# Hybrid diffusion layer on one core: the modulation's rest moved behind the scan, twelve low parts moved to VectorE, shared rows for the exponents

## Chip, cores and metric

One core of a Trainium2 chip runs the whole program. The metric is the device time of one execution in microseconds (us); the kernel before has a median of 1192.13 us over three runs (1191.94 to 1193.13). Engines: TensorE (PE), VectorE (DVE), ScalarE (ACT), GpSimd (POOL) and SyncE (SP), whose queue issues all DMAs.

## What is computed

One layer over 512 latent tokens and 256 context tokens of width 1024, all in float32:

```python
shift1, scale1, gate1, shift2, scale2, gate2 = jnp.split(c_mod[:, None, :], 6, axis=-1)
h = modulate(rms_norm(x, norm1), shift1, scale1)
u = h @ w_in                                   # q, k, v of A and C, z, xbc, dt of B, three gates
...
xs, bm, cm, dt = ssm_inputs(lat('b_xbc'), lat('b_dt'), ssm_conv_w, ssm_conv_b, ssm_dt_bias)
yf, _ = ssd_scan(xs, dt[:, :, 0], a_coef[0], bm, cm, hf_c, True)
yb, _ = ssd_scan(jnp.flip(xs, 1), jnp.flip(dt[:, :, 1], 1), a_coef[1],
                 jnp.flip(bm, 1), jnp.flip(cm, 1), hb_c, True)
ys = ssm_output(yf, jnp.flip(yb, 1), xs, lat('b_z'), ssm_d, ssm_norm)
x = x + gate1 * merge_branches(ya, ys, yg, lat('gates'), w_oa, w_ob, w_oc, w_out)
h2 = modulate(rms_norm(x, norm2), shift2, scale2)
x = x + gate2 * conv_ffn(h2, ffn_w_up, ffn_w_gate, ffn_conv_w, ffn_conv_b, ffn_w_down)
```

Branch A is sliding-window attention, branch C dense attention, branch B a state-space scan that runs forward and backward over chunks of 128 tokens. c_mod is silu(c) @ w_mod + b_mod: six vectors of 1024. shift1 and scale1 are needed first; gate1, shift2, scale2 and gate2 ("the rest of the modulation") are needed only after the three branches are merged.

## The kernel before

Every matrix product is made of three float32r products: each operand is split into a high and a low part (hi and lo, `split`), and hi x hi, hi x lo and lo x hi are summed in PSUM. For weights `wchunk` loads 128x1024 floats (512 KB) into raw, ScalarE copies them into whi, and raw - whi is written to wlo by VectorE or, where its second argument is `pool`, by GpSimd.

**Order.** The code records operations with `Plan`, which then simulates them with a table of durations (`_Eng`, `HOP`, `RELEASE`) and issues, engine by engine, the order it found. `ph(prio, lane, side, dma)` sets priorities for what is recorded next (TensorE, the other engines, DMAs; a smaller number goes first), and `P.hold` makes operations depend on another one. On the chip each engine, and SP's queue, works through its list strictly in order, and waits where an operand is not there.

**Stages, in the order of the profile's time.**
- 0 to 60 us: first modulation (`mod1`, f32r parts mh and ml), normalization and transposes of x, then k, v and q of branch C (`kv_proj`, `q_proj`) and the context tokens (tiles ch and cl; cl is made by GpSimd).
- to 400 us: attention of C and A (`att_unit`: scores in S, exponentials p, their parts ph and pl, products with V), with the convolved inputs of the scan (`xbc_tile`) and `dt_part` as filler.
- 400 to 560 us: `z_part` (weights' low parts on GpSimd), the chunk states of the scan (tiles H, xwh, xwl, yac) and the first gates of `merge`.
- 560 to 700 us: `scan_g` for two groups of heads and four chunks each. Per half chunk of four heads TensorE computes exponents into S (two matmuls per direction: one of SL with SR, one of idr with a mask), ScalarE takes the exponential E, VectorE and ScalarE scale it and make Mh and Ml, and TensorE multiplies xhl by these. Per chunk VectorE adds the result to yac and multiplies by zg, ScalarE squares it (ssB), TensorE transposes yac, and VectorE makes yn, then yth and ytl.
- 427 to 800 us: `merge` for branches C, A and B: per column block of 128 a gate product (hh, hl with w_g) and an output product (y0, y1, yth, ytl with the branch's weights), into m32. What does not depend on the scan runs beside it.
- 700 to 840 us: merge of B's remaining blocks, w_out, second norm; then the MLP to the end.

**The rest of the modulation.** `mod_rest(gi)` (lines 1024 to 1054) handles one of four vectors in two halves. For each half VectorE forms acc, the sum over eight rows of weights times sc, from four loads mraw of 512 KB, and TensorE sums acc over partitions (with a matrix of ones). The gates (gi 0 and 3) go through DRAM (gsc) and come back as g1 and g2; shift2 and scale2 go to md2. acc and mraw have one buffer each, in the pool wp. For gi 0 to 2 it is called behind `xbc_tile` with `P.hold = {mark[7]}` (the last product of the second unit of C's attention) and priorities 4.5, 2.8, 1.85.

**The exponents.** Two pairs of tiles SR and SL are kept. For each direction, SR has the sums of the four heads in rows 0 and 1 (high and low part) against ones in SL's rows 0 and 1, and SL's rows 2 to 9 have the same sums against -1 in SR, so that their product is the difference of the sums at two positions. They come from DRAM tiles fsc0 and fsc1:

```python
for d in range(2):
    f = fsc[d][c, g * 2 + q]
    sync.dma_start(SR[q][0:2, d].bitcast(F32).rearrange("s (h t) -> s h t", h=4), f.rearrange("(s h) t -> s h t", s=2))
    sync.dma_start(SL[q][2:10, d].bitcast(F32), f)
    pe.matmul(ps[:, d], SL[q][:, d], SR[q][:, d], start=True, stop=False)
    pe.matmul(ps[:, d], idr, bc(mkr[:, d], 1, [128, 4, 128]), start=False, stop=True)
```

Of the kernel before, what the change touches and what calls it, by code (L numbers as in the profile page):

```python
# [9 lines left out]
F32 = mybir.dt.float32  # L10
# [369 lines left out]
RELEASE = 0.2  # L380
HX = 0.0
# [21 lines left out]
class _Eng:  # L403
# [3 lines left out]
    def __getattr__(self, m):  # L407
        def call(*args, **kw):
# [9 lines left out]
            if self._n == "pe":  # L418
                n = int(np.prod(out.shape[1:]))
                if m == "transpose" or args[1].dtype == F32:  # L420
                    dur = 109.0 if m == "transpose" else max(108.0, n * 1.667 + 2.5)
                else:
                    dur = max(57.0, n * 0.436 + 4.0)
                if not kw.get("start", True):
                    reads.append(out)
            elif self._n == "dma":
# [3 lines left out]
                dur, lat = n * 4 / 360.0, 2200.0  # L430
            else:
# [18 lines left out]
                if self._n == "act" and "accum_out" in kw:  # L450
                    dur += 205.0
# [14 lines left out]
def emit(tc, A, dbg=None):  # L466
    P = Plan(tc)
# [275 lines left out]
    def kv_proj(br, hold0=set(), hold1=set()):  # L743
        P.hold = hold0
        chs = [wchunk(A["w_kv"][br * 2 + i], pool) for i in range(2)]
# [35 lines left out]
    def q_proj(br, u, early=None):  # L781
        if early is not None:
            ph(QP, "proj", 0.4, early)
        chs = [wchunk(A["w_q"][(br * 2 + u) * 2 + i], pool) for i in range(2)]
# [102 lines left out]
    fsc = [T(dr, [4, 4, 8, 128], F32, f"fsc{d}") for d in range(2)]  # L887
# [56 lines left out]
    def dt_part():  # L944
# [40 lines left out]
        for d, mi in ((0, "U"), (1, "Lo")):  # L985
            pf = bank((128, 4, 128))
            for c in range(4):
                pe.matmul(pf[0:16, c], dA[:, c, d * 16:d * 16 + 16], M[mi], start=c == 0, stop=c == 3)
            fh, fl = ftile((128, 4, 128), F32R), ftile((128, 4, 128), F32R)
            split(fh[0:16], fl[0:16], pf[0:16])  # L990
            for j, f in enumerate((fh, fl)):
                for gq in range(4):
                    sync.dma_start(fsc[d][:, gq, j * 4:j * 4 + 4, :].rearrange("c h t -> h c t"), f[gq * 4:gq * 4 + 4].bitcast(F32))
# [30 lines left out]
    def mod_rest(gi):  # L1024

        for hf in range(2):
            acc = T(wp, [128, 512], F32, "acc", bufs=1)
            for c4 in range(4):
                raw = T(wp, [128, 1024], F32, "mraw", bufs=1)
# [62 lines left out]

    ytp = openp("ytp", bufs=1, side="right")
# [69 lines left out]
    sg1 = T(ss2, [128, 128], F32, "G", bufs=2)  # L1163
    sync.dma_start(sg1, A["segc"][:, 512:640])
# [4 lines left out]
    SR = [T(ss2, [128, 2, 512], F32R, f"SR{i}") for i in range(2)]  # L1169
    SL = [T(ss2, [128, 2, 128], F32R, f"SL{i}") for i in range(2)]  # L1170
    for i in range(2):
        act.activation(SR[i], bc(sgc, 1, [128, 2, 512]), AF.Copy)
        act.activation(SL[i], bc(sg1, 1, [128, 2, 128]), AF.Copy)
    ssB = T(cst, [128, 4, 2], F32, "ssB")
    def scan_g(g):
# [10 lines left out]
        for c in range(4):  # L1186
# [42 lines left out]
            act.activation(zg, y, AF.Square, accum_out=ssB[:, c, g:g + 1])  # L1229

# [72 lines left out]
    closep("ytp")  # L1303
    closep("yp")
# [85 lines left out]

    ap = openp("ap", bufs=1, side="left")
# [5 lines left out]
    mod_rest(3)  # L1397
# [73 lines left out]
def lay_out(x, c, ctx, c_ctx, w_mod, b_mod, norm1, norm2, w_in, a_sink, ssm_conv_w, ssm_conv_b, ssm_A_log, ssm_dt_bias,  # L1471
# [108 lines left out]
```

## Time and profile before

| | |
|---|---|
| median of 3 runs | 1192.13 us |
| the profiled execution: its time, its span | 1197.12 us, 1195.3 us |
| TensorE busy, mean granted clock | 1132.8 us, 0.978 |
| VectorE, ScalarE, GpSimd busy | 809.4, 557.8, 276.9 us |
| DMA | 133.49 MB, mean 112 GB/s |

The time of a run includes a little before and after the span. All rows of the trace come from this one execution. Almost every instruction has the same line (456, where operations are recorded), so tiles tell them apart: b and S are tiles in PSUM, f is the filler's tile, and a name such as b<-whi,hh is output<-inputs. An idle time in brackets is that of the engine before the instruction, with what ended it. The granted clock is a share of TensorE's 2.4 GHz; at the lower of its two levels, 1.2 GHz, it is 0.5.

### The profile page before, as it was taken

How to read it: one execution, taken by the hardware profiler on the slowest of the kernel's cores; microseconds unless marked ns; L12 is line 12 of the kernel's file. 1: busy time of each engine (PE TensorE's matmuls, PEld its weight loads, DVE VectorE, ACT ScalarE, POOL GpSimd, SP SyncE). 2: the span in 40 equal slices, each digit the busy share in tenths (PEclk: the TensorE clock that was granted, in tenths of full speed). 3: DMA queues.
4: the chain of work that ended last, by engine and by line, in shares of the span. 5: the costliest groups of instructions: out<-in, count | busy, mean ns of one | idle time of the engine just before them, and what ended most of it. 6: DMA issues, size and time to landing. Idle time of an engine off the chain costs nothing.

```text
span 1195.3 us, 16560 instructions
## 1 busy us (share of the span) xinstructions
PE 1132.8 (95%) x6218; PEld 956.8 (80%) x6218; DVE 809.4 (68%) x1231; ACT 557.8 (47%) x1017; POOL 276.9 (23%) x181
## 2 busy tenths in 40 slices
PE   6989999899999999999999679999999999999996
PEld 1779888898888998777888568888988888888885
DVE  3788998868997668898898755435865555552423
ACT  4635787347775533435665523236433333332222
POOL 0455232342232453652332200024000000000100
PEclk8999999899999999999999779999999999999999
DMA  8610010331111675546233212352553323233321
GB/s 302 225 62 27 23 63 1 107 124 54 41 54 58 180 239 191 195 153 196 84 113 103 72 53 89 97 185 71 181 171 90 104 90 104 91 123 106 96 80 71
DMA packets 52047, 133.49 MB, mean 112 GB/s; under 512 B 5184, under 2 KB 17600, under 8 KB 51968
## 3 DMA queue, kind: packets, MB, share of 16 engines
q1 hardware_dynamic: 51968, 132.44, 34.1%
q8 instruction: 49, 0.80, 0.3%
q14 instruction: 30, 0.25, 0.1%
HBM read 122.06 MB, written 10.35 MB: 111 GB/s over the span
## 4 chain that ended last, share of the span: by engine, by line
PE 83%; DVE 8%; ACT 4%; issue 2%; DMA 1%; POOL 1%; SPq 0%; POOLq 0%; DVEq 0%; ACTq 0%
PE b L456 73%; PE S L456 11%; DVE pl L456 1%; DVE f L456 1%; DVE st L456 1%; ACT E L456 1%; DVE acc L456 1%; DMA mraw<-in_w_m 1%; DVE y L456 1%; ACT whi L456 0%; DVE yac L456 0%; DVE E L456 0%; DMA m<-in_w_m 0%; DMA SL<-fsc 0%; DVE wlo L456 0%
## 5 line engine op out<-in xcount | busy, mean ns | idle before, releaser
L456 ACT ACTIVATE whi<-raw 128x1024 fp32r<-128x1024 f32 x146 | 154.5, 1059 | 267.7 <-PE b L456 207.1
L456 DVE TENSOR_TENSOR wlo<-raw,whi 128x1024 fp32r<-128x1024 f32 x112 | 140.4, 1254 | 173.8 <-ACT whi L456 173.7
L456 PE MATMUL b<-h2h,whi 128*128 128x512 f32 (+1 forms) x400 | 145.2, 364 | 1.8 <-ACT h2h L456 1.8
L456 PE MATMUL b<-h2l,whi 128*128 128x512 f32 (+1 forms) x400 | 145.5, 364 | 0.6 <-DVE h2l L456 0.5
L456 PE MATMUL b<-h2h,wlo 128*128 128x512 f32 (+1 forms) x400 | 145.8, 366 | 0.0
L456 PE MATMUL b<-hh,whi 128*128 128x512 f32 x288 | 114.4, 397 | 2.1 <-DVE m L456 0.9
L456 PE MATMUL b<-hh,wlo 128*128 128x512 f32 x288 | 114.5, 397 | 0.0
L456 PE MATMUL b<-hl,whi 128*128 128x512 f32 x288 | 114.3, 397 | 0.0
L456 POOL TENSOR_TENSOR wlo<-raw,whi 128x1024 fp32r<-128x1024 f32 x34 | 86.0, 2540 | 112.8 <-ACT whi L456 111.3
L456 PE MATMUL b<-wlo,hh 128*128 128x256 f32 x320 | 92.3, 290 | 1.9 <-POOL wlo L456 1.9
L456 PE MATMUL b<-whi,hh 128*128 128x256 f32 x320 | 93.2, 292 | 0.0
L456 PE MATMUL b<-whi,hl 128*128 128x256 f32 x320 | 92.0, 289 | 0.0
L456 PEld LDWEIGHTS b<-h2h,whi 128*128 128x128 f32 x400 | 75.2, 189 | 14.3 <-ACT h2h L456 2.0
L456 PEld LDWEIGHTS b<-h2l,whi 128*128 128x128 f32 x400 | 75.4, 189 | 12.9 <-DVE h2l L456 1.1
L456 PEld LDWEIGHTS b<-h2h,wlo 128*128 128x128 f32 x400 | 75.3, 189 | 12.4 <-issue 0.5
L456 POOL TENSOR_TENSOR x<-x,fn 128x512 f32<-128x512 f32 x4 | 5.6, 1399 | 293.3 <-ACT f L456 293.3
L456 POOL TENSOR_TENSOR p<-p,st 128x768 f32<-128x768 f32 (+2 forms) x32 | 43.4, 1357 | 119.0 <-DVE st L456 99.3
L456 PEld LDWEIGHTS b<-wlo,hh 128*128 128x128 f32 x320 | 62.6, 196 | 2.6 <-POOL wlo L456 2.1
L456 PEld LDWEIGHTS b<-hh,whi 128*128 128x128 f32 x288 | 54.3, 189 | 13.0 <-DVE m L456 1.3
L456 PEld LDWEIGHTS b<-whi,hl 128*128 128x128 f32 x320 | 62.4, 196 | 0.9 <-issue 0.9
L456 PEld LDWEIGHTS b<-whi,hh 128*128 128x128 f32 x320 | 62.6, 196 | 0.7 <-issue 0.2
L456 PE MATMUL S<-kT,qT 128*128 128x256 f32 (+2 forms) x256 | 61.1, 340 | 2.1 <-ACT p L456 1.2
(287 smaller groups left out, 2866.6 us busy)
## 6 DMA issues: line engine op xcount, KB each, us to landing
mraw<-in_w_m SPq DMA_DIRECT2D x32, 512.0 KB
raw<-in_w_g SPq DMA_DIRECT2D x24, 512.0 KB
raw<-in_w_up SPq DMA_DIRECT2D x22, 512.0 KB
raw<-in_w_gate SPq DMA_DIRECT2D x22, 512.0 KB
raw<-in_w_down SPq DMA_DIRECT2D x22, 512.0 KB
m<-in_w_m SPq DMA_DIRECT2D x16, 512.0 KB
xg<-xsc SPq DMA_DIRECT2D x28, 256.0 KB
raw<-in_w_x SPq DMA_DIRECT2D x12, 512.0 KB
```

What stands on the lines that cost most here:

```text
L456: return f(*[res(a) for a in args], **{k: res(v) for k, v in kw.items()})
```

## The change

Five things are changed. (1) `mod_rest` for gi 0 to 2 is called behind `scan_g`, held until the square of the seventh of eight chunks (`ydone[MH]`), with priorities 6.5, 7.2 and 5.5; its tiles lie in a pool of its own, mrp (m3p for the fourth), with two buffers for mraw. (2) The low parts of the four k, v chunks and eight q chunks are made by VectorE. (3) fsc is one tensor; SR has no direction any more and holds the sums of both directions in rows 0 to 3, SL picks the direction by its ones and zeros; three loads per half chunk and not four. (4) Some of the planner's durations are other numbers. (5) Two small loads use other tiles.

```diff
+MH = 6
+MD = 5.5
...
-                    dur = 109.0 if m == "transpose" else max(108.0, n * 1.667 + 2.5)
+                    dur = 109.0 if m == "transpose" else max(224.0, n * 1.75)
...
-                    dur = max(57.0, n * 0.436 + 4.0)
+                    dur = max(111.0, 120.0 if n == 256 else n * 0.436 + 4.0)
...
-                dur, lat = n * 4 / 360.0, 2200.0
+                dur, lat = n * 4 / 330.0, 2400.0
...
-                    dur += 205.0
+                    dur += 105.0
...
-        chs = [wchunk(A["w_kv"][br * 2 + i], pool) for i in range(2)]
+        chs = [wchunk(A["w_kv"][br * 2 + i]) for i in range(2)]
...
-        chs = [wchunk(A["w_q"][(br * 2 + u) * 2 + i], pool) for i in range(2)]
+        chs = [wchunk(A["w_q"][(br * 2 + u) * 2 + i]) for i in range(2)]
...
-    fsc = [T(dr, [4, 4, 8, 128], F32, f"fsc{d}") for d in range(2)]
+    fsc = T(dr, [4, 4, 16, 128], F32, "fsc")
...
-    def mod_rest(gi):
+    def mod_rest(gi, mrp):
...
-            acc = T(wp, [128, 512], F32, "acc", bufs=1)
+            acc = T(mrp, [128, 512], F32, "acc")
...
-                raw = T(wp, [128, 1024], F32, "mraw", bufs=1)
+                raw = T(mrp, [128, 1024], F32, "mraw", bufs=2)
...
-    P.hold = {mark[7]}
-    ph(4.5, "mod", 2.8, 1.85)
-    for gi in range(3):
-        mod_rest(gi)
-    P.hold = set()
...
-    SR = [T(ss2, [128, 2, 512], F32R, f"SR{i}") for i in range(2)]
+    SR = [T(ss2, [128, 512], F32R, f"SR{i}") for i in range(2)]
...
+                f = fsc[c, g * 2 + q]
+                sync.dma_start(SR[q][0:4].bitcast(F32).rearrange("s (h t) -> s h t", h=4), f.rearrange("(s h) t -> s h t", s=4))
                 for d in range(2):
-                    f = fsc[d][c, g * 2 + q]
-                    sync.dma_start(SR[q][0:2, d].bitcast(F32).rearrange("s (h t) -> s h t", h=4), f.rearrange("(s h) t -> s h t", s=2))
-                    sync.dma_start(SL[q][2:10, d].bitcast(F32), f)
-                    pe.matmul(ps[:, d], SL[q][:, d], SR[q][:, d], start=True, stop=False)
+                    sync.dma_start(SL[q][4 + d * 8:12 + d * 8, d].bitcast(F32), f[d * 8:d * 8 + 8])
+                for d in range(2):
+                    pe.matmul(ps[:, d], SL[q][:, d], SR[q], start=True, stop=False)
                     pe.matmul(ps[:, d], idr, bc(mkr[:, d], 1, [128, 4, 128]), start=False, stop=True)
...
+            ydone.append(P.ops[-1])
...
     for g in range(2):
         scan_g(g)
+    P.hold = {ydone[MH]}
+    ph(6.5, "mod", 7.2, MD)
+    for gi in range(3):
+        mod_rest(gi, mrp)
```

What this makes of the engines' lists is shown at three places. First TensorE at the last half chunk of the scan, in the kernel before: the exponents (SR, idr), the transposes of the chunk before (yac) and the products of the last half (xhl).

```order
L456 MATMUL S_7530<-SR_1228_6331,SL_1230_6341 128x512
L456 MATMUL S_7530<-mkr_6273,idr_6268 128x512
L456 MATMUL S_7530<-SR_1228_6331,SL_1230_6341 128x512
L456 MATMUL S_7530<-mkr_6273,idr_6268 128x512
L456 MATMUL b_7538<-mats_86,yac_5480 128x128 x4
L456 MATMUL S_7521<-xhl_7536,Mh_7561 128x128
```

In the changed kernel:

```order
L458 MATMUL S_7345<-SR_1189_6106,SL_1191_6112 128x512
L458 MATMUL S_7345<-mkr_6070,idr_6065 128x512
L458 MATMUL S_7345<-SR_1189_6106,SL_1191_6112 128x512
L458 MATMUL S_7345<-mkr_6070,idr_6065 128x512
L458 MATMUL b_7355<-mats_86,yac_5417 128x128 x4
L458 MATMUL b_7286<-hl_232,whi_7160 128x512
L458 MATMUL b_7286<-hh_221,wlo_7206 128x512
L458 MATMUL b_7286<-hh_221,whi_7160 128x512
L458 MATMUL b_7286<-hl_232,whi_7160 128x512
L458 MATMUL b_7286<-hh_221,wlo_7206 128x512
L458 MATMUL b_7376<-y_1496_6411,whi_7292 128x512
L458 MATMUL b_7376<-y_1497_6428,whi_7292 128x512
```

Before, the products follow the transposes at once; now 17 matmuls of the merge stand between (the seven shown and ten more of b_7376).

Second VectorE in the same last chunk, in the kernel before, from the squared chunk's neighbour on:

```order
L456 TENSOR_TENSOR E_7544<-E_7544 128x512
L456 TENSOR_TENSOR ytl_7410<-yn_7548,yth_7367 128x4x128
L456 TENSOR_TENSOR E_7544<-E_7544,G_7387 128x512
L456 TENSOR_TENSOR Ml_7563<-E_7544,Mh_7561 128x512
L456 TENSOR_TENSOR yac_5480<-S_7521,yac_5480 128x512 x2
L456 SCALAR_TENSOR_TENSOR yac_5480<-zg_7541,yac_5480 128x512
L456 TENSOR_TENSOR yn_7582<-b_7577,cols_58 128x512
```

In the changed kernel:

```order
L458 TENSOR_TENSOR wlo_7388<-raw_7164,whi_7379 128x1024
L458 TENSOR_TENSOR E_7358<-E_7358 128x512
L458 TENSOR_TENSOR ytl_7182<-yn_7364,yth_7173 128x4x128
L458 TENSOR_TENSOR E_7358<-E_7358,G_7155 128x512
L458 TENSOR_SCALAR acc_7403<-mraw_7367,sc_104 128x512
L458 SCALAR_TENSOR_TENSOR acc_7403<-mraw_7367,sc_104,acc_7403 128x512
L458 TENSOR_TENSOR Ml_7409<-E_7358,Mh_7405 128x512
L458 SCALAR_TENSOR_TENSOR acc_7403<-mraw_7383,sc_104,acc_7403 128x512 x2
L458 TENSOR_TENSOR yac_5417<-S_7335,yac_5417 128x512 x2
L458 SCALAR_TENSOR_TENSOR yac_5417<-zg_7351,yac_5417 128x512
L458 SCALAR_TENSOR_TENSOR acc_7403<-mraw_7411,sc_104,acc_7403 128x512
L458 TENSOR_TENSOR yn_7434<-b_7429,cols_58 128x512
```

The first operations of the moved modulation (acc) and one low part (wlo) now stand in this chain. The last matmul of the modulation stands as the fourth of w_out on TensorE, 312 matmuls of the merge behind the last product of the scan.

Third GpSimd while the context tokens are made (cl), in the kernel before:

```order
L456 TENSOR_TENSOR cl_577<-y_12_538,ch_568 128x256 x2
L456 TENSOR_TENSOR wlo_611<-raw_341,whi_595 128x1024
L456 TENSOR_TENSOR cl_577<-y_12_538,ch_568 128x256 x4
L456 TENSOR_TENSOR wlo_653<-raw_404,whi_643 128x1024
L456 TENSOR_TENSOR cl_577<-y_12_538,ch_568 128x256 x2
```

In the changed kernel:

```order
L458 TENSOR_TENSOR tabs_491<-cs_444,rows_438 128x256 x4
L458 TENSOR_SCALAR tabs_491<-tabs_491 128x512
L458 TENSOR_TENSOR cl_565<-y_12_508,ch_561 128x256 x8
L458 TENSOR_TENSOR hs_501<-hs_501,cols_58 128x4
L458 TENSOR_TENSOR wlo_654<-raw_399,whi_647 128x1024
```

The two low parts of q weights (wlo_611 and wlo_653) are gone from between the eight operations for cl.

## Rows read from the trace of the kernel before

**Rows 1.** The page's first part: busy time, its share of the span, instructions.
```profile
PE 1132.8 (95%) x6218; PEld 956.8 (80%) x6218; DVE 809.4 (68%) x1231; ACT 557.8 (47%) x1017; POOL 276.9 (23%) x181
```

**Rows 2.** Busy time by stretch: each engine's us (instructions), granted clock, DMA share, GB/s.
```profile
210.00:220.00 10.00, 6.23 (x34) 5.11 (x34) 8.32 (x10) 5.34 (x11) 7.12 (x3) 0.76 0.51 148
440.00:450.00 10.00, 8.13 (x53) 7.69 (x52) 4.60 (x3) 1.00 (x2) 3.56 (x2) 0.83 0.61 203
470.00:480.00 10.00, 9.98 (x37) 8.10 (x38) 8.86 (x13) 2.67 (x4) 5.32 (x5) 0.83 0.62 191
80.00:240.00 160.00, 152.66 (x1075) 138.15 (x1075) 139.09 (x252) 103.19 (x208) 54.85 (x31) 0.98 0.15 46
400.00:560.00 160.00, 153.67 (x851) 132.38 (x851) 134.01 (x166) 67.17 (x103) 79.10 (x50) 0.98 0.62 197
560.00:670.00 110.00, 108.51 (x548) 90.23 (x547) 94.08 (x120) 70.16 (x145) 32.65 (x20) 1.00 0.33 104
670.00:703.00 33.00, 16.76 (x52) 12.36 (x51) 18.76 (x30) 12.01 (x28) 6.36 (x5) 0.59 0.10 32
703.00:800.00 97.00, 97.00 (x429) 80.29 (x428) 45.86 (x55) 30.85 (x42) 6.04 (x4) 1.00 0.38 125
```

**Rows 3.** TensorE in order of time, 670 to 703 us: start, duration, [idle <-releaser].
```profile
675.76 0.47 PE L456 MATMUL S<-xhl,Mh 128*128 128x128 f32 x1 [4.93 <-ACT Mh L456]
...
681.05 0.47 PE L456 MATMUL S<-xhl,Mh 128*128 128x128 f32 x1 [2.39 <-DVE xhl L456]
...
689.85 0.48 PE L456 MATMUL S<-xhl,Mh 128*128 128x128 f32 x1 [4.16 <-ACT Mh L456]
...
694.73 1.09 PE L456 MATMUL b<-mats,yac 128*128 128x128 f32 x4 [2.40 <-DVE yac L456]
697.26 1.22 PE L456 MATMUL b<-yth,whi 128*128 128x512 f32 x2 [1.44 <-ACT yth L456]
```

**Rows 4.** The tile acc: ns min/median/max, first and last start; whom VectorE awaited.
```profile
L456 DVE SCALAR_TENSOR_TENSOR acc<-mraw,sc,acc x56: 735/750/2783, 223.8 to 884.5; 128x512 f32<-128x512 f32 x56
...
  DMA mraw<-in_w_m: 7.6, 12
```

**Rows 5.** The tile raw: the low parts on VectorE and on GpSimd.
```profile
L456 DVE TENSOR_TENSOR wlo<-raw,whi x112: 1208/1226/2301, 439.6 to 1170.2; 128x1024 fp32r<-128x1024 f32 x112
L456 POOL TENSOR_TENSOR wlo<-raw,whi x34: 2370/2414/3330, 32.1 to 820.6; 128x1024 fp32r<-128x1024 f32 x34
```

**Rows 6.** SP's queue in order of time, around 445 and 846 us.
```profile
444.97 0.42 SPq L456 DMA_DIRECT2D mraw<-in_w_m  x1
...
846.09 0.33 SPq L456 DMA_DIRECT2D mraw<-in_w_m  x1
```

**Rows 7.** VectorE in order of time, around 213, 452 and 851 us.
```profile
212.88 2.17 DVE L456 TENSOR_TENSOR f<-f,rows 128x192 f32<-128x192 f32 x1
...
220.12 0.36 DVE L456 TENSOR_TENSOR f<-f,f 128x192 f32<-128x192 f32 x1
...
452.34 1.54 DVE L456 SCALAR_TENSOR_TENSOR acc<-mraw,sc,acc 128x512 f32<-128x512 f32 x2 [1.42 <-DMA mraw<-in_w_m]
...
850.76 0.75 DVE L456 SCALAR_TENSOR_TENSOR acc<-mraw,sc,acc 128x512 f32<-128x512 f32 x1 [0.28 <-DMA mraw<-in_w_m]
```

**Rows 8.** TensorE in order of time, 210 to 220 and 440 to 470 us.
```profile
215.83 0.58 PE L456 MATMUL b<-pl,V 128*128 128x256 f32 x1 [2.38 <-DVE pl L456]
...
218.21 0.58 PE L456 MATMUL b<-pl,V 128*128 128x256 f32 x1 [1.16 <-DVE pl L456]
...
443.61 0.39 PE L456 MATMUL b<-wlo,hh 128*128 128x256 f32 x1 [1.87 <-POOL wlo L456]
...
468.71 1.05 PE L456 MATMUL b<-mats,acc 128*128 128x1 f32 x8 [0.63 <-DVE m L456]
```

**Rows 9.** GpSimd in order of time, 205 to 232 us.
```profile
210.14 7.12 POOL L456 TENSOR_TENSOR wlo<-raw,whi 128x1024 fp32r<-128x1024 f32 x3 [2.68 <-ACT whi L456]
```

**Rows 10.** TensorE's waits over the span: total, times, longest.
```profile
PE b L456 <- POOL cl L456: 4.8, 3, 2.3
```

More of the change, by code (lines that the diff above doesn't have):

```diff
@@ L992, in dt_part @@
                 for gq in range(4):
-                    sync.dma_start(fsc[d][:, gq, j * 4:j * 4 + 4, :].rearrange("c h t -> h c t"), f[gq * 4:gq * 4 + 4].bitcast(F32))
+                    sync.dma_start(fsc[:, gq, d * 8 + j * 4:d * 8 + j * 4 + 4, :].rearrange("c h t -> h c t"), f[gq * 4:gq * 4 + 4].bitcast(F32))
         pa, pd, pt2 = bank((128, 6, 32)), bank((128, 6, 32)), bank((128, 6, 32))
@@ L1090, in emit @@
     ph(5, "chain")
+    mrp = openp("mrp", bufs=1, side="right")
     ytp = openp("ytp", bufs=1, side="right")
@@ L1162, in emit @@
     sync.dma_start(sgc, A["segc"][:, 0:512])
-    sg1 = T(ss2, [128, 128], F32, "G", bufs=2)
-    sync.dma_start(sg1, A["segc"][:, 512:640])
+    sg1 = T(ss2, [128, 256], F32, "zg")
+    sync.dma_start(sg1, A["segc"][:, 512:768])
     idr = T(ss2, [128, 128], F32R, "idr")
@@ L1168, in emit @@
     act.activation(mkr, mats[:, 6:8], AF.Copy)
-    SR = [T(ss2, [128, 2, 512], F32R, f"SR{i}") for i in range(2)]
+    SR = [T(ss2, [128, 512], F32R, f"SR{i}") for i in range(2)]
     SL = [T(ss2, [128, 2, 128], F32R, f"SL{i}") for i in range(2)]
     for i in range(2):
-        act.activation(SR[i], bc(sgc, 1, [128, 2, 512]), AF.Copy)
-        act.activation(SL[i], bc(sg1, 1, [128, 2, 128]), AF.Copy)
+        act.activation(SR[i], sgc, AF.Copy)
+        act.activation(SL[i].rearrange("p d t -> p (d t)"), sg1, AF.Copy)
     ssB = T(cst, [128, 4, 2], F32, "ssB")
+    ydone = []
     def scan_g(g):
@@ L1303, in emit @@
     closep("ytp")
+    closep("mrp")
     closep("yp")
@@ L1388, in emit @@
     closep("hp")
+    m3p = openp("m3p", bufs=1, side="left")
     ap = openp("ap", bufs=1, side="left")
@@ L1396, in emit @@
     ph(7.5, "mod", 8.5)
-    mod_rest(3)
+    mod_rest(3, m3p)
     P.hold = set()
@@ L1554, in lay_out @@
     m["mR"] = np.where(q <= r, f32(0), f32(NEG))
-    sg = np.zeros((128, 640), f32)
-    for j in range(2):
+    sg = np.zeros((128, 768), f32)
+    for j in range(4):
         for h in range(4):
-            sg[2 + j * 4 + h, h * 128:(h + 1) * 128] = -1.0
-    sg[0:2, 512:640] = 1.0
+            sg[4 + j * 4 + h, h * 128:(h + 1) * 128] = -1.0
+    for d in range(2):
+        sg[2 * d:2 * d + 2, 512 + d * 128:640 + d * 128] = 1.0
     A["segc"] = sg
```

## The prediction

> **What bounds the kernel now.** I read the page's first part, then busy time by stretch, then each engine in order of time where TensorE stops. TensorE is busy for 1132.8 of 1195.3 us [rows 1]. Every matmul is issued from one fixed list, so the end is the work of that list plus what it waits plus what a lower clock costs. No matmul is added or removed here, so only the last two can move.
>
> The stretches [rows 2] show where they lie. From 560 to 670 us TensorE works 108.51 of 110 us, from 703 to 800 all 97. Between them, in the last chunks of the scan (670 to 703), it works 16.76 of 33 us and the mean granted clock is 0.59, so most of it is at 1.2 GHz and not at 2.4. In order of time [rows 3] the reader sees why: the exponents of a chunk are on TensorE, then ScalarE and VectorE turn them into Mh and Ml, and nothing else is left that TensorE could do. The waits of the two chunks are 4.93 and 2.39 us, then 4.16, 2.40 and 1.44.
>
> What makes the scan end so late is VectorE: 134.01 of 160 us busy from 400 to 560, against 45.86 of 97 from 703 to 800 [rows 2].
>
> **Part 1, the modulation.** The modulation's weights are taken up in 64 operations (56 that add to acc, at a median 0.75 us [rows 4], and 8 that begin one); three quarters move, 48: 36 us of VectorE. In the kernel before nearly all of them stand between 400 and 560 us; VectorE's waits for the weights, 7.6 us in 12 waits [rows 4], mostly go from there too. In the changed order they begin inside the last scan chunk and end at the first matmuls of w_out.
>
> *What it gives.* The scan reaches its last chunks with matmuls of the gates still unspent. By the order there are 17 of them between the exponents and the products of the last chunk where there was none. One costs 97 us / 429 = 0.226 us [rows 2], so 17 cover 3.9 us. A stall of 4 to 5 us before Mh would close, but the same piece of the order puts a wlo (1.2 us, [rows 5]) and two acc operations in front of Ml, and two more acc in front of the yac additions: 1.2 + 4 x 0.75 = 4.2 us. So I leave the last chunk's stalls as they are (4.16 + 2.40 + 1.44 = 8.0 us) and strike those of the chunk before it, which now has its own gate matmuls between exponents and products: 16.24 us idle become 8. Of the 16.76 us at the lower clock, which cost 16.76 / 2 = 8.4 us, half go with them: 4.2. Together **-12 us**. Bounds: 0 if the filler is eaten by a slower VectorE, -24.6 (16.24 + 8.4) if all closes.
>
> *What it costs.* From the end of the scan to the last modulation matmul the list holds 312 matmuls of the merge, 312 x 0.226 = 70 us. The first weights are asked for up to one chunk earlier (14 us, from 675.76 to 689.85 [rows 3]; I take 12), so 24 loads of 512 KB have about 82 us. VectorE has room: 45.86 / 97 of 82 us is 39, and 36 more make 75. The loads are the doubt. From its issue to VectorE's use one took 4.67 us (846.09 to 850.76), another 7.37 us where 203 GB/s moved (444.97 to 452.34) [rows 2, 6, 7]. With two buffers and 1.5 us of use, 24 loads take 24 x (4.67 + 1.5) / 2 = 74 us or 24 x (7.37 + 1.5) / 2 = 106 us: nothing exposed or 24 us. The new stretch moves more than 203 GB/s, but its loads are spread by the list where those stood in a heap; I take 5.7 us, a third of the way, so 86 us against 82: **+4 us**, bounds 0 and +24. What is late then stands ahead of everything: weights behind these loads on SP's queue, wlo behind acc on VectorE, TensorE behind both.
>
> *What else it leaves.* At 468.71 TensorE waited 0.63 us and then ran eight one-column matmuls of the modulation in 1.05 us [rows 8]; the clock of 470 to 480 is 0.83 [rows 2], 1.7 us lost. At 443.61 it waited 1.87 us for a wlo of z on GpSimd, which stays there, and 440 to 450 lost another 1.7 us. Of these 6 us I count the first group and a little of the second, as VectorE no longer crowds that stretch: **-4 us**, bounds -6 and 0.
>
> **Part 2, the low parts.** Twelve operations (4 of k and v, 8 of q) leave GpSimd, 2.414 us each, for VectorE, 1.226 us each [rows 5]: 29.0 us less there, 14.7 more here. VectorE has little room in this stage, 139.09 of 160 us [rows 2], so by that alone up to 14.7 us could come out. But the trace shows what GpSimd's three did to VectorE: while they ran (210.14 to 217.26, [rows 9]) a 128x192 operation with two inputs took 2.17 us that otherwise takes 0.36 [rows 7], and ended with the second of the three. TensorE waited for pl behind it, 2.38 and 1.16 us [rows 8], and 210 to 220 ran at 0.76 [rows 2], another 2.4 us. All three are of the moved kind, and a moved one holds VectorE for half the time. So I cost the 14.7 us at nothing: they are covered by the time for which VectorE no longer stands behind GpSimd. If that cover were gone they would cost up to 14.7 us. The stall and its clock go: **-6 us**, bounds -6 and 0. In the context tokens TensorE waited 4.8 us for cl in three waits [rows 10]; on GpSimd two q parts stood among the eight cl, and now none does. VectorE's copies ahead of cl stay, so I take less than half: **-2 us**, bounds -4.8 and 0.
>
> A rule speaks against this part. The Trainium skill, Perfetto Trace Analysis, Optimizing Scalar/DVE Operations, advises that with VectorE saturated some of its work may go to ScalarE or even GPSIMD, while warning that the port shared by GPSIMD and VectorE can spoil it. By the advice the move goes the wrong way, which is the third rival below; by the warning it is neutral or better, and the rows above, where GpSimd's work lengthened VectorE's, are of that kind.
>
> **Part 3, the shared rows.** Per half chunk one load of SR replaces two, and SR's first fill has 512 columns and not 1024; the matmuls are the same. No wait for SR or SL stands among TensorE's stalls of [rows 3], so 0.
>
> **Part 4, the planner's numbers.** New durations reorder everything by a few matmuls. I cost this at 0 with +-5 us, about the size of the small waits that no part above touches.
>
> **Sum.** -12 + 4 - 4 - 6 - 2 = -20 us. The profiled execution took 1197.1 us (span 1195.3), 5 us over the median 1192.13; I take the difference off the median: 1192.1 - 20 = **1172 us**, and a profiled span near 1175. The terms' likely errors give 1164 to 1180 for this case alone.
>
> **Rivals.**
> - *All of the scan's end closes* (chance 0.14). For it: 17 matmuls are nearly the length of the stall. Against: the acc operations in that chain. The tail then keeps 2 us and not 8 + 4.2: 1172 - 10 = 1162; with the planner's numbers helping, 1158.
> - *The scan's end does not shrink* (0.14). The filler moves but VectorE is as late as before, because the scan itself holds 94.08 of 110 us of it [rows 2]. Term -12 becomes 0: 1184. This is also the case in which the change does not do what it says.
> - *VectorE becomes the bound of the attention* (0.10). The 14.7 us come out by half, 7.4, and the 8 us of part 2 are not gained: 1172 + 15 = 1187. Against: in [rows 7, 9] VectorE waits for GpSimd, not the other way.
> - *The modulation's loads arrive late* (0.10), the case that ends slower. At 7.37 us each, 24 us are missing between the scan and w_out; they show as waits of about 3 us in each of the eight column blocks of the merge, some long enough for the lower clock, as at 215.83 [rows 8], say 4 us: 1172 - 4 + 24 + 4 = 1196. It decides from a landing of about 5.3 us on, where (5.3 + 1.5) / 2 x 24 passes 82 us, and turns the gain to a loss at about 7 us. For it: the stretch must carry 12.6 MB more in 82 us on top of 125 GB/s, some 280 GB/s, more than 400 to 560 had (197) [rows 2].
>
> **How the numbers follow.** The forecast has 0.52. The range must hold 8 in 10: it takes in the forecast's own range, all closing, no shrinking and most of the attention case, and leaves out the late loads and the outer edges: 1158 to 1187. A measurement of this kernel tells about 0.2% (2.4 us) from no change. Slower by more: most of the late loads and a little of the attention case, 0.11. Within 0.2%: the rest of those two, 0.04. Faster: 0.85.
>
> **What would show it.** Right: in the changed profile the stretch of the last scan chunks has one group of waits (Mh, Ml, yac, yth) of about 8 us and not two; 210 to 220 and its waits for pl are gone; the z and state stage has no acc on VectorE; the 70 us after the scan show acc without TensorE stalls over 1 us. Wrong: TensorE waiting for acc, wlo or m after the scan; VectorE's wait for mraw above 10 us; more waits for pl, p or V before 400 us; a clock under 0.9 in any 100 us that had 1.00.

## The result, and the profile after

The changed kernel took 1164.98 us (median of 4 runs, 1162.62 to 1165.41) against 1192.63 for the kernel before: a ratio of 0.9764 (95% interval 0.9747 to 0.9781), or 27.6 us less. 1172 was forecast, with 1158 to 1187 as the range.

The page's first part for the changed kernel ([rows 1] for the kernel before):

```profile
PE 1121.2 (96%) x6218; PEld 949.7 (82%) x6218; DVE 793.3 (68%) x1243; ACT 556.2 (48%) x1017; POOL 241.3 (21%) x169
```

Busy time by stretch, with the columns of [rows 2]. The stretches are cut where the same work now lies; the scan's end, 670 to 710 before, is now 640 to 670.

```profile
60.00:80.00 20.00, 17.15 (x130) 15.83 (x130) 15.33 (x33) 7.10 (x13) 9.88 (x11) 1.00 0.18 53
80.00:240.00 160.00, 157.73 (x1148) 145.28 (x1148) 135.82 (x252) 105.45 (x211) 37.74 (x23) 1.00 0.13 42
400.00:560.00 160.00, 158.85 (x844) 135.59 (x843) 115.14 (x138) 78.34 (x133) 77.60 (x52) 1.00 0.44 138
...
640.00:650.00 10.00, 7.15 (x34) 5.67 (x33) 7.72 (x12) 4.91 (x10) 2.80 (x2) 0.88 0.62 198
650.00:660.00 10.00, 6.16 (x18) 4.58 (x18) 7.96 (x16) 1.35 (x3) 1.38 (x1) 0.50 0.53 152
660.00:670.00 10.00, 10.00 (x39) 7.42 (x38) 7.65 (x12) 4.79 (x7) 0.00 (x0) 0.94 0.46 163
...
670.00:780.00 110.00, 109.19 (x503) 90.08 (x502) 75.40 (x113) 34.83 (x53) 8.63 (x8) 1.00 0.58 195
780.00:810.00 30.00, 27.32 (x199) 25.73 (x198) 19.48 (x30) 15.52 (x31) 10.65 (x7) 0.94 0.41 139
```

Two numbers per stretch can be read from such rows: TensorE's idle time (length less busy time), and what the lower clock cost (busy time x (1 - granted clock), summed over windows of 10 us, as the three from 640 to 670 show). In us:

| work | before: idle + clock | after: idle + clock | change | term of the prediction |
|---|---|---|---|---|
| start, 0 to 60 | 11.6 + 3.0 | 11.4 + 3.1 | 0 | none |
| context tokens, 60 to 80 | 4.8 + 0 | 2.9 + 0 | -2.0 | -2 |
| attention, 80 to 240 | 7.3 + 2.5 | 2.3 + 0 | -7.6 | -6 |
| 240 to 400 | 3.1 + 0 | 2.6 + 0 | -0.5 | none |
| z, states, 400 to 560 | 6.3 + 3.1 | 1.2 + 0 | -8.3 | -4 |
| scan, up to its last chunks | 1.5 + 0 | 1.5 + 0 | 0 | none |
| end of the scan (670 to 710; now 640 to 670) | 16.2 + 7.4 | 6.7 + 4.5 | -12.4 | -12 |
| merge, w_out, norm (710 to 840; now 670 to 810) | 2.3 + 0 | 3.5 + 1.5 | +2.7 | +4 |
| MLP | 9.3 + 0 | 9.8 + 0.1 | +0.6 | none |
| sum | 78.4 | 51.0 | -27.5 | -20 |

The sum agrees with the medians. The two profiled spans differ by 32.3 us; the profiled execution of before was 5 us above its median, and those 5 us are spread over TensorE's busy time and can't be placed.

TensorE in order of time at the new end of the scan, columns as in [rows 3]:

```profile
647.72 0.47 PE L458 MATMUL S<-xhl,Mh 128*128 128x128 f32 x1 [2.20 <-ACT Mh L458]
648.84 0.48 PE L458 MATMUL S<-xhl,Ml 128*128 128x128 f32 x1 [0.65 <-DVE Ml L458]
...
652.99 1.08 PE L458 MATMUL b<-mats,yac 128*128 128x128 f32 x4 [2.40 <-DVE yac L458]
655.52 1.22 PE L458 MATMUL b<-yth,whi 128*128 128x512 f32 x2 [1.45 <-ACT yth L458]
```

One group of waits is left where there were two: 6.7 us (8.0 were forecast for it). Its wait for Mh is 2.20 us where it was 4.16, because the 17 merge matmuls now run ahead of it.

The tile acc, as in [rows 4]: the first addition now starts at 647.4 us, not at 223.8, no operation is longer than 0.753 us (2.783 before), and VectorE's waits for the loads are 6.0 us in 8 waits, from 7.6 in 12.

```profile
L458 DVE SCALAR_TENSOR_TENSOR acc<-mraw,sc,acc x56: 736/750/753, 647.4 to 834.1; 128x512 f32<-128x512 f32 x56
...
  DMA mraw<-in_w_m: 6.0, 8
```

TensorE's waits over the span (total, times, longest): acc appears with 1.2 us, and pl and cl, 5.6 and 4.8 us before, are no longer among the first eleven.

```profile
PE b L458 <- DVE yac L458: 2.8, 2, 2.4
PE S L458 <- ACT Mh L458: 2.2, 1, 2.2
...
PE b L458 <- DVE acc L458: 1.2, 3, 0.7
```

So the total lies in the range, 7 us beyond the forecast, and four of the five terms came out within 2 us of their sizes. The experiments ask whether the parts did it for the stated reasons.

### The profile page after: what moved, and what is told of

Read it like the earlier page. It is cut to its first block, busy times and chain, and to the rows that moved or that the text cites. A ratio compares the mean times of both kernels' runs of the same rounds, so it can differ in the third digit from the quotient of the medians.

```text
span 1163.0 us, 16557 instructions
## 1 busy us (share of the span) xinstructions
PE 1121.2 (96%) x6218; PEld 949.7 (82%) x6218; DVE 793.3 (68%) x1243; ACT 556.2 (48%) x1017; POOL 241.3 (21%) x169
## 4 chain that ended last, share of the span: by engine, by line
PE 81%; DVE 11%; ACT 3%; issue 3%; DMA 2%; POOL 0%; SPq 0%; POOLq 0%; DVEq 0%; ACTq 0%
PE b L458 71%; PE S L458 10%; DVE st L458 2%; DVE pl L458 1%; DVE y L458 1%; DMA mraw<-in_w_m 1%; DVE acc L458 1%; DVE wlo L458 1%; DVE f L458 1%; DVE E L458 1%; ACT whi L458 1%; DVE p L458 0%; ACT E L458 0%; DVE Ml L458 0%; DMA m<-in_w_m 0%
## 5 line engine op out<-in xcount | busy, mean ns | idle before, releaser
L458 DVE TENSOR_TENSOR wlo<-raw,whi 128x1024 fp32r<-128x1024 f32 x124 | 157.4, 1271 | 186.0 <-ACT whi L458 182.9
L458 PEld LDWEIGHTS b<-h2l,whi 128*128 128x128 f32 x400 | 76.3, 191 | 12.4 <-DVE h2l L458 0.6
L458 POOL TENSOR_TENSOR wlo<-raw,whi 128x1024 fp32r<-128x1024 f32 x22 | 53.0, 2412 | 106.4 <-ACT whi L458 105.1
L458 PEld LDWEIGHTS b<-hl,whi 128*128 128x128 f32 x288 | 54.2, 188 | 9.6 <-issue 0.2
L458 PEld LDWEIGHTS b<-hh,wlo 128*128 128x128 f32 x288 | 54.2, 188 | 9.6
```

Source lines behind the costliest of these rows:

```text
L458: return f(*[res(a) for a in args], **{k: res(v) for k, v in kw.items()})
```

## Experiments

"Before" is the kernel before on the same chip. Two kinds of kernel occur: those planned anew, where one part changes the whole list; and those in which the planner's order is kept row for row and only an engine, some work or the place of a few operations is changed when it is issued.

### The low parts alone, order kept (e_wlo_pin)

The kernel before, its order kept; the chunks of k, v and q are recorded with SWAP on, and their low parts go to VectorE:

```diff
-            f = getattr(self._r, m)
+            sw = SWAP[0] and self._n == "pool" and m == "tensor_tensor"
+            f = getattr(self._p.dve._r if sw else self._r, m)
...
-                q = last.get(o.eng)
+                q = last.get(o.real)
```

> The kernel before with the twelve low parts of q, k and v planned on GpSimd as they were and only issued on VectorE: TensorE's, ScalarE's and SP's lists are those of before, row for row. Theory (part 2 by its own mechanism): the waits for pl at 215 us (2.38 and 1.16 us) and the clock loss behind them go, and about half of the 4.8 us of waits for cl; -8 us, 1184 to 1185 us, and VectorE's operations around 213 take 0.36 us again, not 2.17. Rival (the gain in that stage comes from the new order, not from the engine): 0, 1192 +-2 us. Rival (VectorE bounds the attention): 7 to 15 us more, 1199 to 1207 us, with new waits of TensorE for pl, p or V.

Measured: 1192.42 us, ratio 0.9982 (0.9968 to 0.9997), 2.1 us less. VectorE around 210 us, then TensorE (start, duration), then the window:

```profile
209.89 0.36 DVE L458 TENSOR_TENSOR f<-f,rows 128x192 f32<-128x192 f32 x1
210.16 1.22 DVE L458 TENSOR_TENSOR wlo<-raw,whi 128x1024 fp32r<-128x1024 f32 x1
211.41 0.69 DVE L458 TENSOR_TENSOR pl<-b,ph 128x512 fp32r<-128x512 f32 x1
```

```profile
212.16 0.39 PE L458 MATMUL b<-pl,V 128*128 128x256 f32 x1 [1.70 <-DVE pl L458]
214.23 0.40 PE L458 MATMUL b<-pl,V 128*128 128x256 f32 x1 [1.34 <-DVE pl L458]
```

```profile
210.00:220.00 10.00, 6.96 (x42) 6.49 (x41) 9.60 (x21) 2.33 (x6) 0.00 (x0) 0.83 0.52 198
```

The operation that took 2.17 us takes 0.36 again, as forecast, and the stall stays all the same: 3.04 us instead of 3.54. VectorE has lost GpSimd's disturbance and gained three operations of 1.22 us. The 2.1 us are about what cl gains: between 60 and 80 us TensorE is idle 2.3 us, from 4.8. So the first theory falls (the engine was not what held TensorE there), and so does the third, with 7 to 15 us lost; the second, that the order matters and not the engine, comes closest.

### The planner's durations alone (e_plan)

The four changed numbers of `_Eng`, in the kernel before; two of them:

```diff
-                    dur = max(57.0, n * 0.436 + 4.0)
+                    dur = max(111.0, 120.0 if n == 256 else n * 0.436 + 4.0)
...
-                    dur += 205.0
+                    dur += 105.0
```

> The kernel before with the planner's new durations alone. Theory (parts 1 and 2 make the gain): 0 +-5 us, 1188 to 1198 us, and the two groups of waits at the end of the scan are still there (16 us of idle TensorE). Rival (the new order by itself carries a good part of the gain): 1184 us or less.

Measured: 1198.68 us, ratio 1.0041 (1.0027 to 1.0055), 4.9 us more. TensorE's longest new wait, and the one at the scan's end:

```profile
75.92 0.47 PE L456 MATMUL b<-mats,qhl 128*128 128x128 f32 x1 [5.80 <-ACT qhl L456]
...
692.63 0.47 PE L456 MATMUL S<-xhl,Mh 128*128 128x128 f32 x1 [5.13 <-ACT Mh L456]
```

Just outside the 1188 to 1198 us expected: alone, the new durations make a worse list. TensorE is idle 6.9 us between 60 and 80 us (4.8 before). At the end of the scan it is idle only 11.8 us (16.2 before), with no move of the modulation at all.

### The move alone, with the shared rows (e_mod2f)

The kernel before with all of the diff but the low parts and the durations:

```diff
+    P.hold = {ydone[MH]}
+    ph(6.5, "mod", 7.2, MD)
+    for gi in range(3):
+        mod_rest(gi, mrp)
...
+                    pe.matmul(ps[:, d], SL[q][:, d], SR[q], start=True, stop=False)
```

The shared rows halve the two SR tiles (from 2 x 4 KB a partition to 2 x 2 KB), and a second mraw buffer takes 4 KB: one pays for the other.

> The kernel before with the modulation moved (two load buffers) and the shared rows, which make the room for the second buffer; low parts and planner's durations as before. Theory: the end of the scan gives about 12 us, the stretch from 400 to 560 us 4 to 8, the loads behind the scan cost 3 to 4: 1192.6 - 12 - 6 + 3 = about 1177 us, and the stall at 215 us stays. Rival (the move needs the new durations to work): 1187 us or more, with two groups of waits at the end of the scan. Rival (the loads are late without the other parts): 1190 us or more, with waits for acc or wlo behind the scan.

Measured: 1185.74 us, ratio 0.9935 (0.9917 to 0.9953), 7.8 us less, half of what was expected.

```profile
670.24 0.47 PE L458 MATMUL S<-xhl,Mh 128*128 128x128 f32 x1 [4.95 <-ACT Mh L458]
...
712.28 1.02 PE L458 MATMUL b<-mats,acc 128*128 128x1 f32 x8 [1.74 <-DVE acc L458]
...
751.13 1.02 PE L458 MATMUL b<-mats,acc 128*128 128x1 f32 x8 [1.42 <-DVE acc L458]
```

The second group of waits at the scan's end is gone here too (10.7 us idle, from 16.2), but the last chunk waits 4.95 us for Mh, and behind the scan TensorE waits for acc, as in the fourth rival, with 3.2 us in place of 24.

### The shared rows alone (e_fsc)

The kernel before with the one tensor fsc, three loads per half chunk and the smaller fill:

```diff
-    SR = [T(ss2, [128, 2, 512], F32R, f"SR{i}") for i in range(2)]
+    SR = [T(ss2, [128, 512], F32R, f"SR{i}") for i in range(2)]
```

> The kernel before with the shared rows of the exponents alone (three loads per half chunk, not four; half the first fill). Theory (part 3 costs and brings nothing by itself; it makes room for the second load buffer): within 2 us of before, 1190 to 1195 us. Rival (fewer loads and a smaller fill shorten the scan): 1189 us or less, and a shorter wait for Mh in the last chunks.

Measured: 1194.38 us, ratio 1.0011 (0.9998 to 1.0023): no difference that the runs can tell. As forecast, the part does nothing by itself.

### The low parts back on GpSimd, order of the changed kernel kept (u_wlo_pin)

The same swap the other way, in the changed kernel:

```diff
+            sw = SWAP[0] and self._n == "dve" and m == "tensor_tensor"
+            f = getattr(self._p.gps._r if sw else self._r, m)
```

> The changed kernel, planned as it is, but its twelve low parts of q, k and v issued on GpSimd: TensorE's, ScalarE's and SP's lists are those of the changed kernel, row for row. The opposite swap, in the order of before, gave 2.1 us, and the wait for pl stayed (1.70 and 1.34 us) with VectorE 9.60 of 10 us busy. Theory now (the order made with the new engines, not the engine, removes the stalls between 80 and 240 us): little, 1165 to 1169 us, the most of it for cl (2.5 us). Rival (in this order the engine matters as part 2 said): 6 us or more slower, 1171 us or more, with waits for pl of over 1 us.

Measured: 1173.17 us, ratio 0.9837 (0.982 to 0.9854), 8.2 us more than the changed kernel. TensorE, then GpSimd:

```profile
71.22 0.39 PE L460 MATMUL b<-whi,cl 128*128 128x256 f32 x1 [2.33 <-POOL cl L460]
```

```profile
208.37 4.72 POOL L460 TENSOR_TENSOR wlo<-raw,whi 128x1024 fp32r<-128x1024 f32 x2 [5.67 <-ACT whi L460]
229.80 2.40 POOL L460 TENSOR_TENSOR wlo<-raw,whi 128x1024 fp32r<-128x1024 f32 x1 [16.70 <-ACT whi L460]
```

So in this order the engine is worth 8 us, as the rival had it, but not where part 2 put them. Idle and clock loss grow by 2.4 us up to 60 us, by 3.8 from 60 to 80 (cl, and 2.5 us of clock) and by 1.3 from there to 400; the end of the scan has 1.2 us less, and some 2.7 of the 7.7 us between the two spans lie in TensorE's busy time and can't be placed. pl is not among TensorE's longer waits. Here GpSimd has two low parts at 208 us and the third 16.7 us behind their end, where [rows 9] has three on end: the new order has no stall at 215 us with either engine, the old one has it with both.

### Low parts, durations and move, each undone and planned anew (u_wlo, u_plan, u_mod)

Each is the changed kernel with one part of the diff taken back: the second argument `pool` of the two `wchunk` calls; the four durations; or `mod_rest` at its old place with one buffer:

```diff
-        chs = [wchunk(A["w_q"][(br * 2 + u) * 2 + i]) for i in range(2)]
+        chs = [wchunk(A["w_q"][(br * 2 + u) * 2 + i], pool) for i in range(2)]
```

```diff
-                    dur = max(111.0, 120.0 if n == 256 else n * 0.436 + 4.0)
+                    dur = max(57.0, n * 0.436 + 4.0)
```

```diff
+    P.hold = {mark[7]}
+    ph(4.5, "mod", 2.8, 1.85)
+    for gi in range(3):
+        mod_rest(gi)
```

> The changed kernel with the twelve low parts on GpSimd, planned anew. Theory (the planner knows the engines and orders the attention around them): the waits for pl come back, 5 to 10 us slower, 1170 to 1176 us. Rival (only the move of the modulation and the durations matter): 1165 +-3 us.

> The changed kernel with the planner's old durations, planned anew. By themselves the new durations made the kernel before 4.9 us slower. Theory (parts work together: the list is only as good as the durations it is made with, once the modulation no longer fills 400 to 560 us): slower than the changed kernel by 5 to 15 us, 1170 to 1180 us, with more waits before 560 us. Rival (the durations add nothing or harm here too): 1160 to 1167 us. The four parts alone sum to -4 us, so some 23 us lie in their interplay; this run and the next say with which part.

> The changed kernel with the modulation back at its old place and one load buffer. Theory (the move gives about 20 us here: tail 12, 400 to 560 us 8): 1183 to 1188 us, with about 16 us of waits in two groups at the end of the scan. Rival (the move's own share is what it gave alone, 8 us): 1173 us.

Measured: u_wlo 1189.33 us (ratio 0.9971, 0.9956 to 0.9987), u_plan 1179.20 (0.988, 0.9861 to 0.9899), u_mod 1179.64 (0.9889, 0.9874 to 0.9904). The first lies 13 us above what was expected, the third 3 below; the second is in its range. With the runs above, and the start of the scan's first exponents in each profile:

| parts (the shared rows in every kernel with the move, and in u_mod) | us to before, by the ratio | scan begins at |
|---|---|---|
| none | 0 | 562.9 |
| durations (e_plan) | +4.9 | 574.1 |
| move (e_mod2f) | -7.8 | 538.5 |
| move, durations (u_wlo) | -3.5 | 545.3 |
| move, low parts (u_plan) | -14.3 | 528.9 |
| low parts, durations (u_mod) | -13.2 | 551.0 |
| all (the changed kernel) | -28.1 | 525.0 |

The parts do not add. The move gives 7.8 us alone and 14.9 as the last part. The durations cost 4.9 alone and give 13.8 as the last part. The low parts give 24.6 as the last part, three times their worth in a kept order. u_wlo waits like e_plan in its first part (columns: start, duration):

```profile
75.46 0.48 PE L458 MATMUL b<-mats,qhl 128*128 128x128 f32 x1 [5.79 <-ACT qhl L458]
...
222.55 0.38 PE L458 MATMUL b<-pl,V 128*128 128x256 f32 x1 [1.97 <-DVE pl L458]
```

and its scan begins 20.3 us later than the changed kernel's, where it has 21.2 us more of idle time and clock loss up to there. The durations make a good list of the first 400 us only with the low parts on VectorE, and the low parts are worth most with the durations. u_mod has that good first part (2.9 us idle from 60 to 80, 2.3 from 80 to 240) and the old end of the scan:

```profile
664.50 0.47 PE L458 MATMUL S<-xhl,Mh 128*128 128x128 f32 x1 [2.39 <-DVE xhl L458]
673.29 0.47 PE L458 MATMUL S<-xhl,Mh 128*128 128x128 f32 x1 [4.16 <-ACT Mh L458]
678.17 1.09 PE L458 MATMUL b<-mats,yac 128*128 128x128 f32 x4 [2.40 <-DVE yac L458]
```

with 13.5 us idle there against 6.7 (the sum of its waits from 659 us on). That difference, with the clock, is the move's as the last part.

### What the modulation costs in either place (a_nomod, b_nomod)

42 of the 48 operations on acc and 18 of the 24 loads of gi 0 to 2 are skipped when the kept order is issued; each acc is then its first product alone.

```diff
+            if getattr(o, "drop", False):
+                continue
...
+                DROP[0] = gi < 3 and c4 > 0
                 sync.dma_start(raw, A["w_m2"][(gi * 2 + hf) * 4 + c4])
...
+                    DROP[0] = gi < 3 and k > 0
```

> The changed kernel, planned as it is, with 42 of the 48 moved operations on acc and 18 of their 24 loads left out (each acc is then its first product alone, so gate1, shift2 and scale2 are not the reference's); the rest of every engine's list is the same. It prices the modulation where it now stands. Theory (behind the scan it is nearly free: 0.65 us in front of Ml, 0.7 us in the merge): 1161 to 1164 us, and the other waits at the end of the scan (2.20, 2.40, 1.45 us) stay. Rival (its loads and its 31 us of VectorE crowd the merge, as the fourth rival of the prediction had it): 1157 us or less, with fewer waits between 700 and 800 us.

> The kernel before, planned as it is, with the same 42 operations and 18 loads left out at the old place. It prices the modulation there, with no new filler for the end of the scan. Theory (the modulation makes VectorE late from 400 to 560 us and no more): the waits and the low clock of that stretch go in part, 9.4 us at most; 1184 to 1189 us, and the two groups of waits at the end of the scan stay (16 us). Rival (it was free there too, and the move gains by the filler and the new order alone): 1190 to 1193 us. Rival (VectorE's lateness reaches into the end of the scan): under 1180 us.

Measured: a_nomod 1161.61 us (ratio 0.9725, 0.9709 to 0.9741), 3.4 less than the changed kernel by the medians (4.7 by the two ratios); b_nomod 1192.40 (ratio 0.9977, 0.9964 to 0.999), 2.7 less than before. a_nomod at the scan's end, TensorE and then the windows:

```profile
647.91 0.33 PE L461 MATMUL S<-xhl,Mh 128*128 128x128 f32 x1 [2.23 <-ACT Mh L461]
...
652.03 1.09 PE L461 MATMUL b<-mats,yac 128*128 128x128 f32 x4 [2.40 <-DVE yac L461]
654.56 1.22 PE L461 MATMUL b<-yth,whi 128*128 128x512 f32 x2 [1.44 <-ACT yth L461]
```

```profile
640.00:650.00 10.00, 7.00 (x37) 5.45 (x36) 6.14 (x10) 5.13 (x11) 2.80 (x2) 1.00 0.55 186
650.00:660.00 10.00, 6.52 (x20) 4.70 (x21) 4.92 (x11) 2.26 (x4) 1.02 (x1) 0.66 0.00 0
```

and b_nomod:

```profile
671.73 0.48 PE L459 MATMUL S<-xhl,Mh 128*128 128x128 f32 x1 [4.94 <-ACT Mh L459]
...
685.81 0.47 PE L459 MATMUL S<-xhl,Mh 128*128 128x128 f32 x1 [4.16 <-ACT Mh L459]
```

Of the modulation's price in the changed kernel, 3.4 us, 2.5 lie at the scan's end (640 to 670 us): 0.2 of idle time (6.5 us for 6.7; 0.40 us are left of the wait for Ml) and 2.3 of clock, as far as single profiles tell. The merge (670 to 810) has 0.9, nearly all of it idle time. So the operations that add to acc are not what holds the last chunk: without them TensorE waits as long. And 31 us of VectorE less at the old place (42 x 0.75), in the old order, bring 2.7 us and leave both groups of waits as they were: the rival's 1190 to 1193 us, not the theory's 1184 to 1189. Most of the move's gain does not come from VectorE having less to do before the scan; it comes with the list made again, in which matmuls are left for the end.

### What holds the last chunk (t_later, t_later2)

In the changed kernel VectorE waits for a weight chunk and makes its low part before it scales E (columns as in [rows 7]):

```profile
643.95 1.25 DVE L458 TENSOR_TENSOR wlo<-raw,whi 128x1024 fp32r<-128x1024 f32 x1 [0.99 <-ACT whi L458]
645.12 0.68 DVE L458 TENSOR_TENSOR E<-E 128x512 f32<-128x512 f32 x1
```

t_later takes the planned order and sets this whi and wlo behind the last Ml; t_later2 sets them behind the last yac, ytl behind the scaling of E, and two acc behind Ml:

```diff
+    def later(self, order):
...
+        order = self.move(order, [wh, wl], yz)
+        order = self.move(order, [yl], eg)
+        return self.move(order, ac, ml)
...
     def issue(self, order):
+        order = self.later(order)
```

> The changed kernel with one weight chunk's high part (ScalarE) and low part (VectorE) issued behind Ml of the last half chunk and not ahead of the scaling of E; the load behind them and nothing else moves with them. In the changed kernel VectorE waits 0.99 us for that high part and works 1.25 us on the low part before it scales E, and TensorE then waits 2.20 us for Mh. Theory (these two operations hold the last chunk, and no longer the lack of filler): the wait for Mh falls below 0.5 us, 2 to 4 us less with the clock: 1161 to 1163 us. Rival (the chain of E itself is that long): the wait stays near 2 us, 1165 us.

> The changed kernel with three shifts inside the last half chunk and the rest of every list kept: the weight chunk's high and low part stand behind the yac additions (the run before put them in front of these, where they made the waits for yac and yth 3.15 and 2.32 us), ytl stands behind the scaling of E, and the two acc operations behind Ml. Theory (the time of the chunk's own chain on VectorE decides, and every other operation put into it is paid for): the waits for Mh and Ml fall to 0.5 us together, those for yac and yth stay at 2.4 and 1.45, 2 to 3 us less with the clock: 1162 to 1163 us. Rival (the granted clock falls there anyway and takes back what the idle time gives): 1164 to 1166 us.

Measured: t_later 1164.95 us (ratio 0.9749, 0.9731 to 0.9767), no difference; t_later2 1162.12 (ratio 0.9741, 0.9726 to 0.9757), whose interval overlaps that of the changed kernel, while its profiled span is 2.9 us shorter (1160.1). t_later, then t_later2:

```profile
647.80 0.33 PE L479 MATMUL S<-xhl,Mh 128*128 128x128 f32 x1 [1.07 <-ACT Mh L479]
...
653.66 1.08 PE L479 MATMUL b<-mats,yac 128*128 128x128 f32 x4 [3.15 <-DVE yac L479]
657.06 1.22 PE L479 MATMUL b<-yth,whi 128*128 128x512 f32 x2 [2.32 <-ACT yth L479]
```

```profile
646.01 0.33 PE L493 MATMUL S<-xhl,Mh 128*128 128x128 f32 x1 [0.61 <-ACT Mh L493]
...
651.63 1.09 PE L493 MATMUL b<-mats,yac 128*128 128x128 f32 x4 [3.90 <-DVE yac L493]
654.60 1.22 PE L493 MATMUL b<-yth,whi 128*128 128x512 f32 x2 [1.88 <-ACT yth L493]
```

The waits move from Mh to yac and yth; their sum is 6.7 us in the changed kernel (2.20 + 0.65 + 2.40 + 1.45), 7.3 and 6.8 here (with 0.80 and 0.40 for Ml). In this chunk VectorE's operations form one chain, and in both shifts what is taken out of one gap fills the next. t_later2's time is the one its theory gave, but not by its mechanism: yac and yth were to stay at 2.4 and 1.45 us. Neither shift nor a_nomod (6.5 us) closes the waits; whether more matmuls for TensorE would was not run. Of the 2.9 us by which t_later2's span is shorter, 2.3 are clock at the scan's end.

## Why the prediction was right, and where its reasons fell

**The scan's end, -12: right in size and in its main step.** The first group of waits closed and the second stayed, 6.7 us for 8.0; the clock gave 2.9 us for 4.2. (Its 8.4 us took all 16.76 us for the lower clock; the windows from 670 to 710 lost 7.4.) u_mod, without the move, keeps both groups, and b_nomod shows that freeing VectorE without the new list does not close them. But the term is not the move's alone: the durations by themselves take 16.2 us of idle time to 11.8 (e_plan). And the reason given for the second group fails in part. The acc operations in VectorE's chain were to eat the filler; without them 6.5 us stay (a_nomod). Where the prediction said that VectorE's 134 of 160 us "makes the scan end so late", b_nomod shows the smaller part it plays: 2.7 us.

**The modulation behind the scan, +4: near in size, not by its reason.** The 4 us were to be loads that land late. From the first load's issue at 640.5 us to the last operation's end at 736.3 the moved work takes 96 us, where 86 were worked out; but the list, too, comes to its last matmul of the modulation only at 736.4, after 96 us and not 82, and TensorE waits for acc 0.8 us in all, 0.66 at the longest. a_nomod finds 0.9 us of the price in the merge, and the rest of the table's +2.7 there without the modulation. Most of the 3.4 us is clock at the scan's end, which the term did not have. In e_mod2f the waits for acc are 3.2 us: the fourth rival's mechanism is real, but small.

**The stretch from 400 to 560 us, -4: too small, outside its bounds.** -8.3 were measured. "Of these 6 us I count the first group and a little of the second" took two stalls of a long list; nearly all of it went (1.2 us are left), the wait for a wlo of z on GpSimd and the 1.41 us ahead of a yth product too. b_nomod shows that leaving out the operations there closes 2 us of this idle time (4.2, from 6.3) and 1.4 us of clock, so freeing VectorE is worth about the forecast 4; the other 5 us came with the new order. (Of the 48 operations 40 stood here; eight ran from 223 to 247 us.)

**The attention, -6 and -2: right in size, wrong in the cause of the 6.** The step that failed is "they are covered by the time for which VectorE no longer stands behind GpSimd ... The stall and its clock go". e_wlo_pin makes that move alone: the covered time is there, but the three operations fill it, the stall stays at 3.04 us of 3.54, and most of the gain is cl's. u_wlo_pin shows the reverse: with the low parts back on GpSimd the stall doesn't return. In the new order two low parts stand near 208 us and not three; which of its shifts took the stall away is not shown. So the size of the 6 is luck, the more as its clock was taken too high: 2.4 us for 210 to 220 us, where 6.23 us of busy time at 0.76 lose 1.5. The engine is worth 8.2 us in the new order, mostly before 80 us (6.2 us of idle time and clock), where part 2 had only the -2 for cl.

The advice that the prediction held against this part (the Trainium skill, Perfetto Trace Analysis, Optimizing Scalar/DVE Operations: a saturated VectorE may give work even to GPSIMD, though the shared port can spoil it) would have had the move lose time. No run does: both kept orders are faster with VectorE, by 2.1 and by 8.2 us, though VectorE is busy 9.60 of 10 us in one window. It is the page's warning that holds here, not its advice.

**The planner's numbers, 0 +-5: the term that was wrong in kind.** Alone they cost 4.9 us, at the edge of that term; as the last part they give 13.8. A term that stands for itself can't say that. The five terms come near as a reading of the two lists together; they are not the parts' shares. The stretches whose gains were larger than forecast are those that the durations closed: with the old ones (u_plan) TensorE is still idle 7.7 us from 80 to 240 and 6.0 from 400 to the scan, against 2.3 and 1.2. The durations don't do it alone: with them e_plan is idle 9.0 us from 80 to 240, and u_mod, without the move, 5.7 from 400 to the scan.

**The rivals.** All closing did not come, and the two shifts of t_later2 did not bring it. "Does not shrink" fell. VectorE did not bound the attention. Late loads: only as above.

What stays open: why the durations spoil the list when GpSimd has the low parts (the 5.8 us for qhl at 75 us) was not followed through the planner, and whether the low parts planned anew without the other parts gain was not run.

## What to carry to other kernels

Where a planner makes the order, a part of a change has two prices: one in a kept order and one in the list made anew. Price the first from rows, and test it by swapping the engine only when the kept order is issued; for the second, run the parts together and one by one, since they don't add (here -7.8, +4.9 and, in a kept order, -2.1 stand against -28.1 together). And look for work of the bound engine that can be left for the place where it starves: here matmuls of 0.226 us left for the last chunks, 17 of them in the last one, covered waits that 31 us less for VectorE in the old order (b_nomod) left as they were.

## What the hardware showed that was not expected

GpSimd's disturbance and VectorE's own work came out nearly equal. During GpSimd's three low parts VectorE lost 1.8 us on the one operation (2.17 for 0.36) and 1.3 on two TENSOR_SCALAR (1.86 us in before, 0.59 in the changed kernel), 3.1 together; making the three low parts itself takes 3.7 (3 x 1.22).

```profile
215.69 1.86 DVE L456 TENSOR_SCALAR f<-f 128x192 f32<-128x192 f32 x2
```

```profile
205.37 0.59 DVE L458 TENSOR_SCALAR f<-f 128x192 f32<-128x192 f32 x2
```

The Trainium skill, SBUF — State Buffer, Who interferes with whom, has it that the port pair shared by VectorE and GpSimd is an exclusive lock, for VectorE operations with two inputs in SBUF and, in a mode that takes both ports, for TENSOR_SCALAR too, where the loser fully blocks. The rows agree: the operation of 2.17 us ends at 215.05 us, the second low part at 214.89, by thirds of its row. In which mode the TENSOR_SCALAR ran no run shows.

In single profiles, nearly the same idle time cost unlike amounts of clock. The changed kernel is idle 6.7 us at the scan's end and has clocks of 0.88, 0.50 and 0.94 in the three windows above (4.5 us). a_nomod has nearly the same waits at the same times, 6.5 us, and 1.00, 0.66 and 1.00 (2.2 us); t_later2 is idle 6.8 us and has one window under 0.95:

```profile
650.00:660.00 10.00, 6.49 (x19) 4.69 (x20) 8.11 (x16) 2.21 (x4) 1.39 (x1) 0.66 0.74 229
```

which costs 6.49 x 0.34 = 2.2 us, 2.3 less than in the changed kernel. What makes the difference is not shown. The changed kernel's own executions have mean clocks from 0.988 to 0.990, and 0.002 of TensorE's 1121 us is 2.2 us, so much of it may lie between two executions and not between the lists; those of t_later2 have 0.991 to 0.993.
